# A two-block transformer kernel: the mixer's state space half set among its projections, its retention half behind, and the first attention worked by pairs of heads

## The chip, the cores and the metric

The kernel runs on one core of a Trainium2 chip. The metric is the device time of one execution in microseconds (us); the median of several executions counts. The core's engines each work through a list of instructions in order and wait for one another by semaphores: PE (matrix products; it writes to the accumulation memory PSUM), DVE (vectors), ACT (elementwise functions and copies), POOL (GpSimd, which here adds and multiplies on SBUF alone), and SP (which issues DMA transfers).

## The reference

Two blocks run one after the other on 512 tokens of width 1024, with 256 context tokens beside the second. The first has a causal attention of 8 heads with three dilations (taken here as one mask), a spatial gating unit and a mixture of 32 experts. The second has two layers, each with a mixer and an FFN; the first layer's mixer is the one changed. It joins a retention of 8 heads of 64 with a state space scan (SSD) of 8 heads, both in both directions and in chunks of 128 tokens:

```python
q, k, v, g, z, xbc, dt_raw = jnp.split(h @ w_in, IN0_SPLITS, axis=-1)
...
decay = jnp.exp(jnp.where(lower, cum[..., :, None] - cum[..., None, :], -jnp.inf))
scores = jnp.einsum('bhnid,bhnjd->bhnij', qc, kc) * decay
y_intra = jnp.einsum('bhnij,bhnjv->bhniv', scores, vc)
kv_chunk = jnp.einsum('bhnjd,bhnj,bhnjv->bhndv', kc, to_end, vc)
...
y_inter = jnp.einsum('bhnid,bhni,bhndv->bhniv', qc, jnp.exp(cum), s_before)
...
yr = ((yr - mu) * lax.rsqrt(var + EPS)).reshape(b, l, RET_WIDTH) * gn_w.astype(jnp.float32)
yr = yr.astype(g.dtype) * jax.nn.silu(g)
ys = bhld(y_ssd) + d_skip[:, None] * xs
ys = rms_norm(ys.reshape(b, l, SSD_INNER) * jax.nn.silu(z), ssd_norm_w)
return jnp.concatenate([yr, ys], axis=-1) @ w_out
```

The same scan serves retention (a fixed decay for each head and direction) and SSD (a decay that depends on the token). The context's final states are the latent scan's first ones. The context mixer has two chunks (n = 0, 1), the latent mixer four.

## The kernel before

All is fp32. A large product is made of three passes: an operand is cut into a rounded part `h` (ACT casts, tile `wh`) and a rest `l` (DVE subtracts, tile `wl`, line 240), and `mm3` multiplies h·h, h·l and l·h. `gemm_a` goes through column chunks of 512: for each it cuts four weight tiles, and for each 128 tokens (tt) runs 24 matmuls into one bank `ga`. The ring of cut tiles holds four (`NH`), so that the next chunk's cut waits for the last products of this one. A tile framework's list scheduler turns the program into each engine's order; Python generators that are advanced in turn (`interleave`, `fill`) decide only what it is offered and in which sequence.

*First attention* (`block1`, lines 385 to 425, 86 to 155 us). Head by head, query tile by query tile: the matmul `sc`, DVE's mask and maximum, ACT's exponential with its sum; then one reciprocal per head (L399), four normalising products, ten transposes `tpb`, and after each second head the products `pvb`. `fill(FL[3])` puts three pieces of a conditioning product (`adb`) behind each head. Behind it come the projections of u and v (`ga`).

*Mixer* (class `Mixer`, for the context and for the latent tokens). `proj` makes q, k, v (chunks 0 to 2) and the gates g, z (3 and 4), `rope` turns q and k, `steps` makes the SSD's step sizes and decays. `states` makes every chunk's contribution (`kvr` for retention, `kvsb` for SSD) and `carry` runs them forward and back. `inside(n)` makes both halves' weights and the products with the carried state: `ret_s`, `ssd_x` (the decay's exponent, from masks Rf and Rb), `ssd_s`, `ret_i`, `ssd_i`; `gather(n)` multiplies them with the values (`ret_o`, `ssd_o`) and normalises both halves with one power on POOL (`rs_r`, L290); `turn(n)` transposes the result (`ytb`) and cuts it into `yT`, the out projection's operand. `outputs` runs `inside(n)` ahead of `gather(n-1)`. The weight of an SSD chunk, E, needs four steps: ACT's exponential, DVE's product with `ssd_s`, and on POOL Rb (L1303), Rf (L1304) and E (L1312).

In the latent mixer all projections run first, then `spread`, `states` and `outputs`, then the out projection, whose k runs from 0 to 7 (0 to 3 are retention's columns, 4 to 7 SSD's). The context mixer is filler in the MoE, whose expert weights come in through a ring `mw`: each pair of experts advances it by 2.25 steps.

Of the kernel before, what the change touches and what calls it, by code (L numbers as in the profile page):

```python
# [17 lines left out]
P = 128  # L18
D = 1024
# [132 lines left out]
FL = (0, 1, 1, 3, 1)  # L152
# [6 lines left out]
class K:  # L159
# [91 lines left out]
    def gemm_a(self, xT, tts, kt, wsrc, chunks, ps, tag, bufs, evac, kc=2, nb=512, ahead={}):  # L251

        for n in chunks:
            W = ahead[n]() if n in ahead else [self.wsplit(wsrc(n, c), (kc, nb)) for c in range(kt // kc)]
            for tt in tts:
                bank = ps.tile([P, 512], F32, name="ga", tag=tag, bufs=bufs)
                for kk in range(kt):
                    wh, wl = W[kk // kc]
                    k = kk % kc
                    self.mm3(bank[:, :nb], xT(kk, tt), (wh[:, k, :], wl[:, k, :]), kk == 0, kk == kt - 1)  # L260
                evac(bank[:, :nb], tt, n)
                yield
# [47 lines left out]
    def block1(self, mix):  # L310
# [73 lines left out]
        PTs = {}  # L384
        for h in range(8):
            hp, b0 = h // 2, 64 * (h % 2)
            pr = p1.tile([P, 1280], F32, name="pr", tag="pr", bufs=2)
            mx = p1.tile([P, NT], F32, name="mx", tag="mx", bufs=2)
            ls = p1.tile([P, NT], F32, name="ls", tag="ls", bufs=2)
            for qt in range(NT):  # L390
                n = (qt + 1) * P
                sc = ps.tile([P, 512], F32, name="sc", tag="sc", bufs=2)
                self.mm(sc[:, :n], qT[b0:b0 + 64, hp, qt * P:qt * P + P], kT[b0:b0 + 64, hp, :n], True, True)
                pv = pr[:, OFF[qt]:OFF[qt] + n]
                V.tensor_tensor(pv, sc[:, :n], amask[:, 512 - n:], ALU.add)
                V.tensor_reduce(mx[:, qt:qt + 1], pv, AX, ALU.max, negate=True)
                S.activation(pv, pv, AF.Exp, bias=mx[:, qt:qt + 1], accum_out=ls[:, qt:qt + 1])
            ri = p1.tile([P, NT], F32, name="ri", tag="ri", bufs=2)
            V.reciprocal(ri, ls)  # L399
            for qt in range(NT):  # L400
                pv = pr[:, OFF[qt]:OFF[qt] + (qt + 1) * P]
                V.tensor_scalar(pv, pv, ri[:, qt:qt + 1], None, op0=ALU.mult)
            pt = p1.tile([P, 1280], F32, name="pt", tag="pt", bufs=3)
            PTs[h] = pt
            o = 0
            for jt in range(NT):
# [1746 lines left out]
```

## Time and profile before

| | |
|---|---|
| Median of three runs | 2355.48 us (2351.6 to 2362.92) |
| The profiled execution's own time | 2353.49 us |
| Its span in the trace | 2351.7 us |
| PE busy | 2252.5 us (96%) |
| DVE busy | 1423.6 us (61%) |
| ACT busy | 794.9 us (34%) |
| POOL busy | 442.9 us (19%) |
| Mean DMA rate | 144 GB/s |

Times in the trace count from the span's start. PE's busy time is modelled, since its matmuls overlap: one that stands with 0.39 us may be followed by the next after 0.23. A wait is named by the instruction that ended it.

### The profile page before, as it was taken

To read this page: it belongs to the slowest core of one execution; us is meant where nothing else is said; L and a number is where in the kernel's file an instruction comes from. 1 tells how busy PE (TensorE), PEld (TensorE's weight loads), DVE (VectorE), ACT (ScalarE), POOL (GpSimd) and SP (SyncE) were. 2 spreads that over 40 slices of the span, in tenths; PEclk is the share of its full clock that TensorE was granted. 3 is DMA by queue.
4 is the path that set the end of the run, shared out by engine and by line. 5 is a ranking of instruction groups with operands and counts; after the bars stand their busy time and mean duration, and the time that the engine had idled before them with its cause. 6 is when DMAs were issued, how large, how long until landed. Compare 5 with 4: busy or idle time off the path is not lost.

```text
span 2351.7 us, 30149 instructions
## 1 busy us (share of the span) xinstructions
PE 2252.5 (96%) x11748; PEld 1688.6 (72%) x11748; DVE 1423.6 (61%) x2341; ACT 794.9 (34%) x1382; POOL 442.9 (19%) x331
## 2 busy tenths in 40 slices
PE   9999999999979988899999999989999999999998
PEld 7667755534458756688888888877877668888876
DVE  8766743434475577776677753465568765444446
ACT  4344323222253243342211112134446545222222
POOL 0010310232250256410000000531022123000006
PEclk9999999999989997999999999999999999999999
DMA  8655498998853001344344331221100043332230
GB/s 297 217 183 202 182 373 332 371 389 336 310 197 99 30 28 54 125 152 135 122 139 135 126 108 55 65 97 62 60 1 1 1 147 107 106 99 92 87 106 39
DMA packets 99151, 338.91 MB, mean 144 GB/s; under 512 B 14373, under 2 KB 16293, under 8 KB 99002
## 3 DMA queue, kind: packets, MB, share of 16 engines
q1 hardware_dynamic: 94394, 324.33, 39.1%
q0 software_dynamic: 4608, 12.59, 1.5%
q8 instruction: 94, 1.54, 0.3%
q14 instruction: 55, 0.45, 0.1%
HBM read 323.21 MB, written 17.86 MB: 145 GB/s over the span
## 4 chain that ended last, share of the span: by engine, by line
PE 72%; DVE 8%; issue 3%; POOL 2%; ACT 2%; DMA 0%; POOLq 0%; SPq 0%; DVEq 0%; ACTq 0%
PE gb L243 22%; PE ob L243 14%; PE ga L243 10%; PE cb L243 6%; PE gu L243 5%; PE sc L243 3%; PE yb L243 3%; PE ptb L1808 2%; DVE wl L240 1%; POOL rs_r L290 1%; PE kb L243 1%; PE vb L243 1%; PE ntb L920 1%; PE ssd_x L243 1%; PE tpm L687 1%
## 5 line engine op out<-in xcount | busy, mean ns | idle before, releaser
L239 ACT CAST wh<-wr 128x1024 fp32r<-128x1024 f32 (+1 forms) x239 | 249.1, 1048 | 629.1 <-PE gb L243 274.9
L240 DVE TENSOR_TENSOR wl<-wr,wh 128x1024 fp32r<-128x1024 f32 (+1 forms) x235 | 309.2, 1323 | 216.4 <-ACT wh L239 211.8
L243 PE MATMUL gb<-fh,wh 128*128 128x512 f32 x672 | 264.0, 393 | 0.0
L243 PE MATMUL gb<-fh,wl 128*128 128x512 f32 x672 | 263.9, 393 | 0.0
L243 PE MATMUL gb<-fl,wh 128*128 128x512 f32 x672 | 263.7, 392 | 0.0
L243 PE MATMUL ob<-wh,hidh 128*128 128x512 f32 x440 | 173.9, 395 | 4.4 <-DVE gob L1529 3.0
L243 PE MATMUL ob<-wl,hidh 128*128 128x512 f32 x440 | 172.5, 392 | 0.0
L243 PE MATMUL ob<-wh,hidl 128*128 128x512 f32 x440 | 172.3, 392 | 0.0
L1536 DVE TENSOR_TENSOR acc<-acc,ob 128x512 f32<-128x512 f32 x160 | 108.3, 685 | 84.6 <-PE ob L243 84.6
L860 DVE SCALAR_TENSOR_TENSOR adacc<-wr,cond,adacc 128x512 f32<-128x512 f32 x224 | 152.9, 752 | 1.4 <-DMA wr<-in_w_ada 1.4
L243 PEld LDWEIGHTS gb<-fh,wl 128*128 128x128 f32 x672 | 126.2, 188 | 28.7
L243 PEld LDWEIGHTS gb<-fl,wh 128*128 128x128 f32 x672 | 126.2, 188 | 27.7
L243 PEld LDWEIGHTS gb<-fh,wh 128*128 128x128 f32 x672 | 126.2, 188 | 27.4
L243 PE MATMUL gu<-mw,xgT 128*64 128x512 f32 x512 | 124.3, 600 | 0.7 <-issue 0.7
L243 PE MATMUL cb<-fh,wh 128*128 128x256 f32 x416 | 118.0, 284 | 0.0
L243 PE MATMUL cb<-fl,wh 128*128 128x256 f32 x416 | 117.6, 283 | 0.0
L243 PE MATMUL cb<-fh,wl 128*128 128x256 f32 x416 | 117.0, 281 | 0.0
L1538 POOL TENSOR_TENSOR acc<-acc,gate 128x1024 f32<-128x1024 f32 x10 | 28.1, 2811 | 468.1 <-DVE acc L1536 468.1
L290 POOL TENSOR_TENSOR rs_r<-rs_v,mhalf 128x1 f32<-128x1 f32 (+1 forms) x54 | 46.4, 861 | 336.8 <-DVE rs_v L288 336.5
L243 PEld LDWEIGHTS ob<-wh,hidh 128*128 128x128 f32 x440 | 82.6, 188 | 24.8 <-DVE gob L1529 3.2
L1491 DVE TENSOR_TENSOR sg<-sg,gb 128x512 f32<-128x512 f32 x42 | 28.9, 688 | 112.3 <-PE gb L243 112.2
L243 PEld LDWEIGHTS ob<-wh,hidl 128*128 128x128 f32 x440 | 82.7, 188 | 18.3
(666 smaller groups left out, 4891.3 us busy)
## 6 DMA issues: line engine op xcount, KB each, us to landing
mw<-in_w_gu SPq DMA_DIRECT2D x128, 512.0 KB
wr<-in_w_ada SPq DMA_DIRECT2D x96, 512.0 KB
mw<-in_w_dn SPq DMA_DIRECT2D x64, 512.0 KB
wr<-in_w_fg SPq DMA_DIRECT2D x44, 512.0 KB
wr<-in_w_fu SPq DMA_DIRECT2D x44, 512.0 KB
wr<-in_w_fd SPq DMA_DIRECT2D x44, 512.0 KB
wr<-in_w_ret SPq DMA_DIRECT2D x28, 512.0 KB
wr<-in_w_in SPq DMA_DIRECT2D x19, 512.0 KB
```

The source lines that it names most:

```text
L239: self.nc.scalar.copy(h, src)
L240: (eng or self.nc.vector).tensor_tensor(l, src, h.bitcast(F32), ALU.subtract)
L243: self.nc.tensor.matmul(out, lhsT, rhs, start=start, stop=stop, **kw)
L290: nc.gpsimd.tensor_tensor(r, v, self.mhalf[:, :n], ALU.pow)
L687: nc.tensor.transpose(bank[:, k, :], xg[:, (j * 4 + k) * P:(j * 4 + k + 1) * P], self.ident)
L860: V.scalar_tensor_tensor(acc[:, r], W[:, k], s, acc[:, r], op0=ALU.mult, op1=ALU.add)
L920: nc.tensor.transpose(bank[:, j, i * P:i * P + P], hp[i][:, (2 * kk + j) * P:(2 * kk + j + 1) * P], self.ident)
L1491: nc.vector.tensor_tensor(t, t, out[1], ALU.mult)
L1536: V.tensor_tensor(a[:, sl], a[:, sl], ob, ALU.add)
L1538: G.tensor_tensor(a, a, gate(tt), ALU.mult)
L1808: nc.tensor.transpose(bank[:, qt * P:qt * P + P], prs[h][qt][:, kt * P:kt * P + P], K.ident)
```

## The change

Four things are done. (1) The first attention goes by pairs of heads: both heads' `sc` for one query tile stand next to each other, from the longest tile to the shortest, each tile is normalised at once (32 reciprocals), and the transposes (`spread`) and products (`values`) of the pair before stand among the scores of this one. (2) The mixer is split into `ssd()` and `ret()`. (3) In `ret()` both directions lie on the partitions, 64 and 64: k and q are doubled with their decays (`kd` on DVE, `qd` on POOL), the state takes 8 products of 64 columns per chunk, its carry runs forward on POOL and back on DVE, and the product with the carried state is added in PSUM to that with the values, 16 matmuls `ret_o` for a chunk. (4) In the latent mixer `ssd()` is offered among the projections, 2.25 steps to each 128 tokens; the SSD columns are turned, then retention runs; the out projection's k begins with the SSD columns. The masks and E go to a ring of their own of four tiles (`sw`), and the ring `b9` shrinks from 7 tiles to 5.

```diff
-FL = (0, 1, 1, 3, 1)
+FL = (0, 1, 1, (2, 2, 1, 1), 1)
...
+        def scores(p, qt):
+            n = (qt + 1) * P
+            sc = [ps.tile([P, 512], F32, name="sc", tag=tag, bufs=2) for tag in ("sc", "mm")]
+            for c in range(2):
+                r = slice(64 * c, 64 * c + 64)
+                self.mm(sc[c][:, :n], qT[r, p, qt * P:qt * P + P], kT[r, p, :n], True, True)
+            for c in range(2):
...
+                V.tensor_tensor(pv, sc[c][:, :n], amask[:, 512 - n:], ALU.add)
+                V.tensor_reduce(mx, pv, AX, ALU.max, negate=True)
+                S.activation(pv, pv, AF.Exp, bias=mx, accum_out=ls)
+                V.reciprocal(ls, ls)
+                V.tensor_scalar(pv, pv, ls, None, op0=ALU.mult)
...
+        for p in range(5):
+            for i in range(NT):
+                if p < 4:
+                    scores(p, NT - 1 - i)
+                    fill(FL[3][i])
+                if p and i:
+                    spread(p - 1, i - 1)
+                    if i > 1:
+                        values(p - 1, i - 2)
+            if p:
+                spread(p - 1, 3)
+                for jt in (2, 3):
+                    values(p - 1, jt)
...
+        kd = self.doubled(V, "kd", self.k, n, K.kdec)
+        b = self.pst("kvr", "sc")
+        for h in range(8):
+            K.mm(b[:, h * 64:h * 64 + 64], kd[:, h * P:h * P + P], self.v[:, n * 512 + h * 64:n * 512 + h * 64 + 64], True, True)
...
+    def carry_r(self, n, d):
...
+        r = slice(64 * d, 64 * d + 64)
+        E = self.nc.vector if d else self.nc.gpsimd
...
+    def ssd(self):
...
+        for n in range(nt):
...
+            for h in range(8):
+                S.mul(Rf[:, h, :], K.m_le, self.dt[:, n, 0, h:h + 1])
+            G.tensor_tensor(Rb, K.m_gt[:, None, :].to_broadcast([P, 8, P]), self.dt[:, n, 1, :, None].to_broadcast([P, 8, P]), ALU.mult)
+            G.tensor_tensor(Rf, Rf, Rb, ALU.add)
...
+            G.tensor_tensor(E, E, Rf, ALU.mult)
...
+    def ret(self):
...
+            qd = self.doubled(G, "qd", self.q, n, K.qdec)
+            qdT = work("qdT")
+            for hb in range(2):
+                bank = pst("qtb", "tp")
+                for h in range(4):
+                    self.nc.tensor.transpose(bank[:, h * P:h * P + P], qd[:, (4 * hb + h) * P:(4 * hb + h) * P + P], K.ident)
+                S.copy(qdT[:, hb * 512:hb * 512 + 512], bank)
+            yield
+            ob = pst("ret_o", "sc")
+            for h in range(8):
+                o = ob[:, h * 64:h * 64 + 64]
+                K.mm(o, PT[:, h, :], self.v[:, n * 512 + h * 64:n * 512 + h * 64 + 64], True, False)
+                K.mm(o, qdT[:, h * P:h * P + P], self.SBr[:, n, h * 64:h * 64 + 64], False, True)
...
+            V.tensor_reduce(st, ob3, AX, ALU.add)
+            V.tensor_scalar(st, st, 1.0 / 64, None, op0=ALU.mult)
+            V.tensor_tensor(yr3, ob3, st[:, :, None].to_broadcast([P, 8, 64]), ALU.subtract)
+            S.activation(sq, yr, AF.Square)
+            V.tensor_reduce(rr, sq3, AX, ALU.add)
+            rs = K.rstd(rr, self.pool, 8, 1.0 / 64, 1e-6)
+            V.tensor_tensor(yr3, yr3, rs[:, :, None].to_broadcast([P, 8, 64]), ALU.mult)
+            V.tensor_tensor(gn, yr, gn, ALU.mult)
+            if self.lat:
+                self.turn(n, 0)
+            yield
...
+LF = 2.25
...
-        for n in ("smx", "ropew", "q", "k", "v", "xst", "qT", "kT", "wro", "SBs0", "SBs1"):
-            where[n] = (plb, "b9", 7)
...
+        for n in ("q", "k", "xst", "qT", "kT", "SBs0", "SBs1"):
+            where[n] = (plb, "b9", 5)
...
+        def half():
+            yield from lm.steps()
+            yield from lm.ssd()
+        fill = half()
+        interleave(lm.proj(range(3)), fill, LF)
+        run_gen(fill)
...
+        for n in range(NT):
+            lm.turn(n, 1)
...
+        run_gen(lm.ret())
...
-        run_gen(lm.out(res, gt, normed, {0: lambda: wo}))
+        run_gen(lm.out(res, gt, normed, {0: lambda: wo}, ks=[4, 5, 6, 7, 0, 1, 2, 3]))
```

How the engines' orders move is seen at four places; a row is one instruction or a run of like ones (their count behind x), with its line, output, operands and size.

PE in the first attention, before: the second head's scores, one tile after the other from short to long, and then the transposes `tpb` of the head ahead of it.

```order
L243 MATMUL sc<-kT,qT 128x128
L243 MATMUL adb<-wr,cond 32x128 x5
L243 MATMUL sc<-kT,qT 128x256
L243 MATMUL sc<-kT,qT 128x384
L243 MATMUL adb<-wr,cond 32x128 x7
L243 MATMUL sc<-kT,qT 128x512
L243 MATMUL adb<-wr,cond 32x128 x3
L409 MATMUL tpb<-c_ident,pr 128x128
```

At that place in the change, from the second pair's first tile on (`res` is the room of a pair's second head).

```order
L243 MATMUL sc<-kT,qT 128x512
L243 MATMUL adb<-wr,cond 32x128 x9
L243 MATMUL sc<-kT,qT 128x384 x2
L243 MATMUL sc<-kT,qT 128x256
L416 MATMUL tpb<-c_ident,pr 128x128 x4
L416 MATMUL tpb<-c_ident,res 128x128 x4
L243 MATMUL sc<-kT,qT 128x256
L416 MATMUL tpb<-c_ident,pr 128x128 x3
```

Scores of a pair stand beside each other, and the transposes of the pair ahead stand among them. In the latent mixer PE's order before has, for the third chunk, both halves' products together, with the transposes `ytb` of the first chunk between:

```order
L243 MATMUL ssd_s<-bcT 128x128 x2
L243 MATMUL ret_i<-SBr,qT 128x128 x8
L243 MATMUL ssd_i<-SBs_7021,bcT 128x512
L1404 MATMUL ytb<-c_ident,res 128x128 x8
L243 MATMUL ssd_i<-SBs_7021,bcT 128x512
L243 MATMUL ret_o<-v,PT 128x64 x8
L243 MATMUL ssd_o<-xst,E 128x64 x8
```

In the change, PE's rows for the SSD chunk n=1, from its second half of `ssd_x` on, which stand between the second weight chunk's last projection matmul and the third's first:

```order
L243 MATMUL ssd_x<-Rf,c_m_gt 128x512
L243 MATMUL ssd_x<-Rb,c_ustrict_2688 128x512
L243 MATMUL ssd_s<-bcT 128x128 x2
L243 MATMUL ssd_i<-SBs_6730,bcT 128x512 x2
L1438 MATMUL ytb<-c_ident,res 128x128 x4
L243 MATMUL ssd_o<-xst,E 128x64 x8
L243 MATMUL ga<-wh,ah_5646 128x512
```

The products of retention are gone from between `ssd_x` and `ssd_o`; projection matmuls stand on both sides. DVE at the third weight chunk's cuts (`wl`), in the change:

```order
L1359 TENSOR_TENSOR ys<-ssd_o,sint 128x512
L1360 TENSOR_TENSOR ys<-ys,sint 128x512
L1361 TENSOR_TENSOR ys<-ys,res 128x512
L240 TENSOR_TENSOR wl<-wr,wh 128x1024
L289 TENSOR_SCALAR rs_v<-frs 128x1
L1365 SCALAR_TENSOR_TENSOR res<-ys,rs_r,ynw 128x512
L240 TENSOR_TENSOR wl<-wr,wh 128x1024
L1278 TENSOR_TENSOR Rf<-c_utri_2682,latla 128x1024
L240 TENSOR_TENSOR wl<-wr,wh 128x1024 x2
```

Before, no SSD chunk's work stood among these cuts. Last, PE in the second part of the latent mixer in the change, from the end of one chunk's `ret_o` to the start of the next (`qtb` are the transposes of `qd`):

```order
L243 MATMUL ret_o<-v,PT 128x64
L243 MATMUL ret_s<-qT,kT 128x128 x8
L1438 MATMUL ytb<-c_ident,res 128x128 x4
L1402 MATMUL qtb<-c_ident,qd 128x128 x8
L243 MATMUL ret_o<-SBr,qdT 128x64
```

The chunk's `ytb` has moved ahead of the next chunk's `ret_o`; before, `ret_o` and `ssd_o` of the next chunk or two stood ahead of it.

## Rows read from the trace of the kernel before

**Rows 1.** The page's part 4: chain of waits, share of the span by engine.
```profile
PE 72%; DVE 8%; issue 3%; POOL 2%; ACT 2%; DMA 0%; POOLq 0%; SPq 0%; DVEq 0%; ACTq 0%
```

**Rows 2.** Windows by stage: us, busy time (x instructions) by engine, PE clock, DMA.
```profile
86.00:155.00 69.00, 69.00 (x596) 38.03 (x595) 49.13 (x125) 37.30 (x98) 0.00 (x0) 1.00 0.59 200
...
762.00:836.00 74.00, 73.27 (x352) 58.16 (x351) 40.19 (x79) 17.55 (x24) 15.13 (x18) 1.00 0.08 24
...
836.00:959.00 123.00, 100.23 (x507) 72.59 (x506) 99.51 (x152) 47.65 (x128) 78.26 (x48) 0.83 0.17 60
...
959.00:1005.00 46.00, 39.27 (x174) 30.55 (x173) 34.32 (x48) 22.60 (x39) 21.61 (x15) 0.91 0.29 103
```

**Rows 3.** DVE groups, 80 to 160: xcount, busy us, mean ns, idle before.
```profile
L399 DVE RECIPROCAL ri<-ls 128x4 f32<-128x4 f32 x8 | 1.4, 171 | 1.0 <-ACT pr L397 1.0
...
L240 DVE TENSOR_TENSOR wl<-wr,wh 128x1024 fp32r<-128x1024 f32 x4 | 4.8, 1221 | 0.0
```

**Rows 4.** Timeline of PE, end of the first attention: start, length, instruction.
```profile
146.56 0.73 PE L243 MATMUL ga<-wh,xTh 128*128 128x512 f32 x2
...
154.44 0.50 PE L243 MATMUL ga<-wl,xTh 128*128 128x512 f32 x1
```

**Rows 5.** Timeline of PE, latent projections: first matmul, first of the last 24.
```profile
762.54 0.39 PE L243 MATMUL ga<-wh,ah 128*128 128x512 f32 x1
...
829.77 0.39 PE L243 MATMUL ga<-wh,ah 128*128 128x512 f32 x1
```

**Rows 6.** Timeline of the latent mixer: transposes, `kvsb`, one chunk's work.
```profile
835.22 1.03 PE L1156 MATMUL mtb<-c_ident,xsT 128*128 128x128 f32 x8
...
848.83 3.70 PE L243 MATMUL kvsb<-xsd,bt 128*128 128x512 f32 x8 [0.24 <-DVE SBr L1209]
...
875.92 1.12 PE L243 MATMUL ssd_x<-Rf,c_m_gt 128*128 128x512 f32 x2
...
879.70 1.90 POOL L1303 TENSOR_TENSOR Rb<-c_m_gt,latdt 128x1024 f32<-128x1024 f32 x1 [2.21 <-PE ssd_x L243]
...
880.00 1.16 PE L243 MATMUL ret_i<-SBr,qT 64*128 64x128 f32 x16
...
881.09 1.98 PE L243 MATMUL ssd_i<-SBs,bcT 128*128 128x512 f32 x4
...
882.91 1.89 PE L243 MATMUL ret_o<-v,PT 128*128 128x64 f32 x16
...
884.64 1.95 PE L243 MATMUL ssd_o<-xst,E 128*128 128x64 f32 x16
...
884.99 2.35 POOL L1312 TENSOR_TENSOR E<-E,Rf 128x1024 f32<-128x1024 f32 x1
```

**Rows 7.** Timeline of the normalisation: square, waiting transposes, power.
```profile
890.90 0.63 ACT L1366 ACTIVATE sq<-ycat 128x512 f32<-128x512 f32 x1 [8.90 <-DVE ycat L1365]
...
900.36 1.97 PE L1404 MATMUL ytb<-c_ident,res 128*128 128x128 f32 x8 [6.10 <-DVE res L1373]
...
942.02 1.80 POOL L290 TENSOR_TENSOR rs_r<-rs_v,mhalf 128x9 f32<-128x9 f32 x1
```

**Rows 8.** Windows in the latent mixer, columns as in rows 2.
```profile
865.00:876.00 11.00, 5.96 (x29) 3.13 (x25) 10.15 (x13) 0.84 (x3) 8.48 (x6) 0.53 0.00 0
...
896.00:916.00 20.00, 15.64 (x62) 12.47 (x63) 13.90 (x22) 3.91 (x12) 10.69 (x7) 0.50 0.08 27
```

**Rows 9.** Timeline of PE: first out-projection matmul, last transposes of the mixer.
```profile
937.69 0.77 PE L243 MATMUL ga<-wh,yT 128*128 128x512 f32 x1
...
958.55 0.66 PE L1404 MATMUL ytb<-c_ident,res 128*128 128x128 f32 x2 [3.52 <-DVE res L1373]
```

**Rows 10.** Groups of instructions on DVE, 835 to 960.
```profile
L1244 DVE TENSOR_TENSOR SBs<-SBs,stt 128x512 f32<-128x512 f32 x6 | 9.6, 1611 | 0.1
...
L1311 DVE TENSOR_TENSOR E<-E,ssd_s 128x512 f32<-128x512 f32 x8 | 5.2, 679 | 6.2 <-PE ssd_s L243 6.2
```

**Rows 11.** Window in the MoE, columns as in rows 2.
```profile
560.00:570.00 10.00, 10.00 (x69) 6.38 (x69) 7.67 (x17) 2.42 (x5) 1.14 (x1) 1.00 0.44 158
```

More of the change, by code (lines that the diff above doesn't have):

```diff
@@ L249, in mm3, with gemm_a @@
         self.mm(out, A[1], Bm[0], False, stop, **kw)
-    def gemm_a(self, xT, tts, kt, wsrc, chunks, ps, tag, bufs, evac, kc=2, nb=512, ahead={}):
+    def gemm_a(self, xT, tts, kt, wsrc, chunks, ps, tag, bufs, evac, kc=2, nb=512, ahead={}, ks=None):
+        ks = ks or list(range(kt))
         for n in chunks:
@@ L383, in block1 @@
         amask = self.load_const("amask", p1)
[L384 to L406, printed above, removed]
@@ L407, in block1, with spread @@
+        def spread(p, jt):
+            o, w = sum((NT - j) * P for j in range(jt)), (NT - jt) * P
+            for c in range(2):
+                if jt == 0:
+                    PTs[p, c] = p1.tile([P, 1280], F32, name="pt", tag="pt", bufs=3)
                 bank = ps.tile([P, 512], F32, name="tpb", tag="tp", bufs=2)
@@ new lines, in ends, with doubled @@
+    def ends(self, pairs):
+        for t, f in pairs:
+            if self.lat:
+                self.nc.vector.tensor_copy(t, f)
+            else:
+                self.nc.vector.memset(t, 0.0)
+    def doubled(self, eng, name, t, n, dec):
+        o = self.work(name)
+        eng.tensor_tensor(o.rearrange("p (h d e) -> p h d e", d=2, e=64),
+                          t[:, n * 512:n * 512 + 512].rearrange("p (h o e) -> p h o e", o=1, e=64).to_broadcast([P, 8, 2, 64]),
+                          dec[:, :, :, None].to_broadcast([P, 8, 2, 64]), ALU.mult)
+        return o
@@ L1376, in outputs @@
-    def outputs(self, ahead=None):
-        K = self.K
-        if self.lat:
-            ynw = K.bcast(self.I["ynw"], D, K.wp, "ynw", "wr", K.NR)
-        else:
-            ynw = K.spread_row(K.w4("ynw"), self.I["ynw"], lambda: self.pst("ynb", "sc"))
-        o = {}
-        self.masks = {0: self.mask(0)}
-        for n in range(self.nt + 1):
-            if n < self.nt:
-                o[n] = yield from self.inside(n)
-                if n == self.nt - 1 and ahead:
-                    ahead()
-                yield
-            if n >= 1:
-                self.gather(n - 1, o.pop(n - 1), ynw)
-                if self.lat:
-                    self.turn(n - 1)
-                yield
@@ L1408, in out @@
-    def out(self, hs, gt, done=None, ahead={}, plain=(0,), join=True):
+        self.spread_x()
+        yield
+        st = [self.big(f"SBs{j}") for j in range(2)]
+        hn = nt // 2
+        self.SBs = lambda n: st[n // hn].rearrange("p (t g d c) -> p t g d c", t=hn, g=2, d=2)[:, n % hn]
+        self.ends(((self.SBs(0)[:, :, 0], K.fin_s[:, :, 0]), (self.SBs(nt - 1)[:, :, 1], K.fin_s[:, :, 1])))
+        for n in range(nt):
+            self.kv_ssd(n)
+            yield
+        self.weights_row()
@@ L1945, in scan @@
                 yield
-            yield from cm.spread()
-            yield from cm.states()
-            yield from cm.outputs()
+            yield from cm.ssd()
+            yield from cm.ret()
             for n in range(NC_):
-                cm.turn(n)
+                for hb in range(2):
+                    cm.turn(n, hb)
             yield
```

420 lines of the change are left out of this document (193 added, 227 removed).

## The prediction

> **What bounds the kernel now.** I read the page's chain of waits first: the matrix engine (PE) holds 72% of it [rows 1], so only a stage where PE waits, or does work it could leave out, can give time back. The table by stage [rows 2] then shows three such stretches among those the change touches. In the first attention (86 to 155 us) PE is never idle, yet its work there is small operands and filler, and the vector engine (DVE) is busy 49 of 69 us. In 762 to 836 PE runs the latent q, k, v projections without a gap (73.3 of 74). In 836 to 959, the latent mixer proper, PE is busy 100 of 123 at a granted clock of 0.83 and DVE 99.5; its 23 us of idle PE are the slack there is.
>
> The timelines give the marks. The projections start at 762.54, and the last 24 of their 288 matmuls `ga` stand from 829.77 to the first transposes at 835.22 [rows 5, 6], 0.227 us each. In the tail, PE waits 6.10 us for the eight transposes `ytb` of n=0 (from 894.3 to 900.4) [rows 7], and the clock is 0.50 from 896 to 916 and 0.53 from 865 to 876 [rows 8], that is, at the lower of its two levels. The out projection begins at 937.69, and the last `ytb` comes at 958.55, when 62 of the 192 out-projection matmuls are done [rows 9].
>
> **The change part by part.** *First attention.* The same masks, maxima, exponentials and products, but the 8 reciprocals of 128x4 become 32 of 128x1: 24 x 0.17 = 4.1 us more DVE work, against 49.1 [rows 2, 3]. The gain is order. The two heads of a pair stand on different row halves, so their score matmuls can run together, as `ret_i` shows: 16 instructions on alternating halves in 1.16 us [rows 6]. And DVE always finds another head's row to work on. Were DVE fed without a gap from 87 us, its 53.2 us, four weight cuts `wl` of 1.22 among them [rows 3], would end at 140; I take 141.5 for the scores and cuts, and the first 24 `ga` of the next projection are then done by about 150. Now the first stands at 146.56 and 26 are done at 154.44 [rows 4], where 44 would be: 18 x 0.227 = **-4 us**. Bounds: 0 (DVE still idles as long as now) and -8.
>
> *Context mixer, filler in the MoE.* There the weight DMA is the limit as long as PE takes the experts' weights; from 560 to 570 PE does mixer work in their place and the DMA share is 0.44 at 158 GB/s [rows 11]. Those 5.6 us are the most to win there. The new order has more PE work (16 `ret_o` matmuls per n instead of 8 and 8 `ret_i`, 1.73 x 2 against 1.73 + 1.09 [rows 6]), ends one pair of experts earlier, and waits in other places. **-1**, bounds -6 and +5.
>
> *Latent, first part: the whole SSD half among the projections.* To the 72.7 us of projection (762.5 to 835.2) come, per n, `ssd_x` with `ssd_s` 4.08 (875.92 to 880.00), `ssd_i` 1.82 and `ssd_o` 1.9 [rows 6], 4 x 7.8 = 31.1; eight `kvsb` 2 x 3.70; 24 transposes at 1.03 for eight, 3.1 [rows 6]. Sum 114.3: with no wait the last `ga` would end at 876.9. But PE works in order, and `ssd_o` needs E, which GpSimd (POOL) makes through Rb, Rf and E: from Rb's start at 879.70, just behind `ssd_x`, to E's end at 887.34 is 7.6 us [rows 6]. What stands between on PE covers it for n=0 (24 `ga` 5.4, `ssd_s` some 0.5, `ssd_i` 1.8), n=2 and n=3. For n=1 nothing but `ssd_s`, `ssd_i` and four `ytb` stands there (the order ahead of this), 2.8 us: a wait of 5. Before the second and third weight chunks DVE reaches the cuts only behind SSD work (behind the states' carries; behind the three adds and products of n=1, which themselves wait for that `ssd_o`): 0 to 6 us each, I take 3 each, which is two cuts and a product of 0.68 [rows 3, 10]. So 11 us of waits and the last `ga` at **888**.
>
> *Latent, second part: retention.* The `rint` scalings and adds are gone. In front stand 32 `kvr` at 0.22 (`ret_o`'s rate), 32 transposes and 12 `ytb`, about 13 us, with four kd, each as wide as a cut (1.22), copies and the backward carry on DVE beside it, about 18 with them; then the first 16 `ret_o` (3.5): 23 us. After that each n runs a chain that nothing covers. PE's order has `ytb` of n ahead of the transposes `qtb` and `ret_o` of n+1. So between them lie DVE's reduce, scale, subtract, ACT's square (0.63), reduce, rs_v, POOL's rs_r (1.80), two products: 5 x 0.68 [rows 10], two small ones of 0.17 like the reciprocal [rows 3], 0.63, 1.80 [rows 7] and 0.9 for eight hand-overs make 7.1 us, then `ytb` 0.5, `qtb` 1.0, the copy 0.6, `ret_o` 3.5: 12.7 us each for three n, and 7.6 for the last. Sum 23 + 38 + 7.6 = **68**, ending at 956. Behind n=2 and n=3 out-projection matmuls fill the wait, as the first halves of their sums need only the SSD result; in PE's order 47 stand ahead of the last `ytb`, against 62 now, a debt of 15 x 0.227 = 3.4. So 956 + 3.4 against 958.6: **+1**.
>
> So of the 23 idle us of PE little is won: 11 us of waits stand in the first part, and in the second a serial chain of 7 us per n, where before the chunks of both halves overlapped.
>
> *What speaks against it in the skill.* Row: DVE's adds of two SBUF operands beside POOL take 1.61 us, where the products with one PSUM operand of the same shape take 0.68 [rows 10]. The Trainium skill, GPSIMD Engine Reference, section Specifications, says that GpSimd shares its SBUF interfaces with VectorE and contends with VectorE instructions of two SBUF inputs; the trace agrees. The cuts that PE waits for in the first part are of that kind. [...]
>
> **The sum.** -4 - 1 + 1 = -4. From the profiled 2353.5 that is 2349.5; the profiled execution lies 2.0 under the median of the three runs, so a median by the same steps is 2351. A difference under 0.5% (11.8 us) can hardly be told from none in this kernel.
>
> **The rivals.** *The waits aren't there (faster).* E may come early where POOL is free, and the cuts may find DVE free: then the last `ga` ends at 877 (-11); kd and the carries of the first chunks may be done before, and the head of the second part falls by 6; attention gives its -8. -4 - 11 - 6 - 4 = -25, from either 2353.5 or 2355.5: **2328 to 2331**. For it: from 762 to 1005 PE's modelled work is 213 of 243 us [rows 2], so about 26 are there to win and no more. Against it: in an engine that works in order the wait of n=1 can't be passed by the matmuls behind it.
>
> *PE falls to its lower clock (slower).* Every wait of 5 to 6 us in the tail now is followed by a stretch at 0.50 to 0.53 [rows 7, 8]; in 896 to 916 PE gets its 15.6 us of work through at half speed, so some 7 us are lost behind one wait. The Trainium skill, TensorE: Matmul & The Clock Gate, section HAM oscillation, describes the same pattern of short work between waits that never regains the clock; the trace agrees. If the three waits of the first part cost 4 each so (+12), and in the second part n=1 and n=2 run `ytb`, `qtb` and `ret_o` at half rate (2 x 5) with the head slower by 3 (+13): -4 + 25 = +21, **2374 to 2376**. It slows the kernel past the 0.5% where the last `ytb` comes after some 972 (958.6 + 11.8 + 5 of attention and context, less the 3.4).
>
> *It moves work and nothing else (same).* Attention gives 0, since the exponentials and transposes set its pace; the context mixer's new waits cost the DMA 5: **2358 to 2360**.
>
> **How the numbers follow.** The forecast (2340 to 2358, latent mixer even, attention a few us) 0.35; the last rival 0.07; the waits that aren't there 0.36; the clock 0.22. The forecast's lower end passes the 0.5% bound (2343.7) with some 0.04 of its chance. So faster 0.40, same 0.38, slower 0.22. The range runs from 2328 to 2376, the two rivals' prices; the forecast's own is 2340 to 2358. Between the two sums I give **2350**.
>
> **What would show it.** In the changed kernel: the first `ga` after the attention by 145 us, with 44 done at 154.4. The last projection `ga` near 888 (877: the first rival; 898: the clock), and a PE wait of some 5 us at the second chunk's `ssd_o` released by POOL's E. Four `ytb` in the second part, each released by DVE's product with `gn` some 7 us after `ret_o`, and spaced by 12 to 13 us; the last at 956. A granted clock under 0.6 in these stretches speaks for the slower rival. The prediction is wrong if projections and SSD work run without PE idle, or if the retention's chunks turn out to overlap, or if the FFN's first matmul `cb` moves by other than the last `ytb` does.

## The result, and the profile after

The changed kernel takes 2425.23 us (median of 4 runs, 2422.58 to 2429.83) where the kernel before takes 2356.28 (4 runs, 2351.6 to 2362.92): a ratio of 1.0293, 95% interval 1.0263 to 1.0322. It is slower by 69 us, outside the range of 2328 to 2376. The profiled execution took 2425.33 us, with a span of 2423.6 (before: 2351.7).

The chain of waits of the changed kernel barely moves against [rows 1]:

```profile
PE 71%; DVE 7%; issue 4%; POOL 2%; ACT 2%; DMA 1%; POOLq 0%; SPq 0%; DVEq 0%; ACTq 0%
```

The place shows in the windows by stage, columns as in [rows 2]. The first four are the windows of [rows 2], the last three this kernel's own stages: the first part from the first projection `ga` to the last, the second to the last `ytb`, and the tail to the FFN's first `cb`:

```profile
86.00:155.00 69.00, 68.21 (x627) 35.50 (x626) 51.65 (x153) 39.07 (x100) 0.00 (x0) 1.00 0.64 214
762.00:836.00 74.00, 58.72 (x246) 40.12 (x245) 45.21 (x79) 22.09 (x42) 12.77 (x12) 0.86 0.11 36
836.00:959.00 123.00, 104.91 (x471) 80.68 (x469) 85.71 (x102) 42.50 (x99) 65.54 (x42) 0.85 0.11 35
959.00:1005.00 46.00, 32.91 (x158) 30.73 (x158) 17.07 (x25) 5.65 (x10) 7.03 (x4) 0.50 0.07 24
...
773.00:928.00 155.00, 128.28 (x514) 89.28 (x513) 95.97 (x145) 51.98 (x120) 63.23 (x45) 0.88 0.14 45
928.00:1021.00 93.00, 71.86 (x397) 65.33 (x395) 49.62 (x62) 17.18 (x29) 25.65 (x17) 0.65 0.11 40
1021.00:1074.00 53.00, 41.23 (x182) 31.73 (x180) 36.92 (x47) 22.16 (x39) 24.32 (x18) 0.90 0.31 109
```

From 762 to 836 PE was busy throughout before and is now idle for 15 us; from 959 to 1005 it runs at the lower clock. The marks of one profiled run of each kernel, read as first and last starts of the matmuls of a tile, give the lengths of the stages (all in us; "first `gu`" is where the experts begin, "experts" reaches to the last `gu`, "part 1" from the first latent `ga` to the last, "part 2" to the last `ytb`, "tail" to the first `cb`). In the kernels with the old latent mixer part 1 is the projections and part 2 the whole mixer. Single marks scatter: PE's order up to the first `gu` is the same in all kernels with the new attention, and yet that mark stands anywhere from 299.5 to 307.8:

```
kernel       median   first gu  experts  part 1  part 2  tail   sum of the three
before       2356.28    304.5    308.1    72.5   125.1   44.2   241.8
after        2425.23    303.6    319.4   154.7    93.3   52.8   300.8
e1_att       2345.23    299.5    308.4    72.4   124.7   44.3   241.4
e2_ctx       2362.70    307.9    320.4    72.3   130.7   40.0   243.0
e3_lat       2407.49    304.9    308.5   157.5    91.7   52.4   301.6
e5_attctx    2358.83    300.7    323.4    72.3   130.9   40.0   243.2
e6_ring      2408.39    300.8    324.9   132.7    95.0   53.1   280.8
e7_rope      2406.89    302.2    321.6   134.8    97.4   53.5   285.7
e8_seq       2425.42    300.4    323.4    83.0   164.7   52.7   300.4
e9_sw        2399.35    300.7    321.6   134.6    88.7   53.0   276.3
e4_late      2402.60    300.2    324.1   153.1    67.3   52.1   272.5
e13_two      2382.76    299.8    321.7   134.2    69.9   52.3   256.4
e10_three    2387.28    306.5    324.3   132.2    77.0   54.6   263.8
e12_attlat   2365.56    301.8    311.0   130.6    70.7   54.5   255.8
e14_pad      2419.39    307.8    322.9   152.5    89.7   51.8   294.0
e15_cheap    2353.91    300.0    316.4    72.4   130.8   40.0   243.2
```

Of the 71.9 us between the two spans the latent stage holds 59.0 and the experts' stage 11.3; the rest nearly cancels. What PE waits for in part 1 (engine, tile, line, releaser: us, times, longest):

```profile
PE kvsb L243 <- DVE xsd L1241: 12.1, 2, 8.9
PE ssd_o L243 <- POOL E L1334: 11.3, 3, 6.1
PE ga L243 <- ACT wh L239: 1.4, 1, 1.4
```

And from SP's list from 740 on the loads of raw weights and of the row of norm weights, first in the kernel before, then in the changed one (start, time from the first issue to the last, load, count):

```profile
743.10 46.11 SPq L223 DMA_DIRECT2D wr<-in_w_ret  x7
...
849.07 0.38 SPq L192 DMA_DIRECT2D ynw<-in_ynw  x1
```

```profile
742.68 0.33 SPq L223 DMA_DIRECT2D wr<-in_w_ret  x1
804.03 0.33 SPq L192 DMA_DIRECT2D ynw<-in_ynw  x1
822.45 66.92 SPq L223 DMA_DIRECT2D wr<-in_w_ret  x8
```

Where seven loads of raw weights were issued between 743 and 789, one is now, and the next begins at 822. SP's own waits in the changed kernel, from 740 to 1060, say why:

```profile
...
SPq L223 <- DVE ys L1360: 70.0, 4, 35.3
SPq L192 <- DVE q L1165: 60.9, 1, 60.9
SPq L223 <- DVE wl L240: 28.3, 4, 15.1
SPq L223 <- DVE q L1165: 18.0, 1, 18.0
```

The ring of six tiles for raw weights, which held the row of norm weights before too, now also holds the mixer's work tiles but Rf, Rb and E: the rope's `ropew`, and of the SSD half `xsd`, `sts`, `sint` and `ys` (the account of the change names only the ring of the masks and E). SP issues in order: it stood 60.9 us until a rope tile was free (its last reader is the add into `q`, L1165) to load `ynw`, and the weights stood behind that load, another 18.0 us for the next rope tile.

How the ring reaches PE shows in the timeline of the changed kernel ahead of its longest wait:

```profile
803.47 0.42 DVE L1165 TENSOR_TENSOR q<-ropew 128x256 f32<-128x256 f32 x1
803.80 2.49 DVE L1241 TENSOR_TENSOR xsd<-xst,latex 128x512 f32<-128x512 f32 x4
...
816.92 0.58 ACT L1141 COPY q<-ga 128x512 f32<-128x512 f32 x1 [4.63 <-PE ga L243]
...
819.36 5.73 POOL L1414 TENSOR_TENSOR res<-res,ynw 128x512 f32<-128x512 f32 x4
819.43 1.47 DVE L1164 TENSOR_TENSOR q<-ropew 128x256 f32<-128x256 f32 x1 [0.61 <-POOL ropew L1163]
820.83 1.48 DVE L1165 TENSOR_TENSOR q<-ropew 128x256 f32<-128x256 f32 x1
822.23 4.62 DVE L1241 TENSOR_TENSOR xsd<-xst,latex 128x512 f32<-128x512 f32 x4
...
825.79 6.17 PE L243 MATMUL kvsb<-xsd,bt 128*128 128x512 f32 x8 [8.91 <-DVE xsd L1241]
```

The rope of the last `q` tile stands ahead of the second half of `xsd` in DVE's list and waits for that tile's projection; next in PE's list is `kvsb`, which waits for `xsd`. The late row's four products on POOL fall there too: beside them the add into `q` takes 1.48 us where it took 0.42 and four `xsd` 4.62 where they took 2.49. The second weight chunk's first `ga` follows at 833.37, behind `kvsb` and a wait of 1.4 us for its cut. So it is by `xsd` that the ring costs PE most; for the weights themselves PE waits 1.9 us in this part.

### The profile page after: what moved, and what is told of

Same layout as the page of the kernel before. It is cut to its first block, busy times and chain, and to the rows that moved or that the text cites. A ratio compares the mean times of both kernels' runs of the same rounds, so it can differ in the third digit from the quotient of the medians.

```text
span 2423.6 us, 30296 instructions
## 1 busy us (share of the span) xinstructions
PE 2290.7 (95%) x11844; PEld 1715.9 (71%) x11844; DVE 1438.4 (59%) x2330; ACT 800.5 (33%) x1379; POOL 440.0 (18%) x327
## 4 chain that ended last, share of the span: by engine, by line
PE 71%; DVE 7%; issue 4%; POOL 2%; ACT 2%; DMA 1%; POOLq 0%; SPq 0%; DVEq 0%; ACTq 0%
PE gb L243 21%; PE ob L243 14%; PE ga L243 10%; PE cb L243 6%; PE gu L243 5%; PE sc L243 3%; PE yb L243 2%; PE ptb L1842 2%; DVE wl L240 1%; PE ret_o L243 1%; POOL rs_r L291 1%; PE kb L243 1%; PE vb L243 1%; PE ssd_x L243 1%; PE ssd_o L243 1%
## 5 line engine op out<-in xcount | busy, mean ns | idle before, releaser
L243 PE MATMUL gu<-mw,xgT 128*64 128x512 f32 x512 | 132.0, 599 | 2.5 <-DMA mw<-in_w_gu 1.0
L1525 DVE TENSOR_TENSOR sg<-sg,gb 128x512 f32<-128x512 f32 x42 | 28.9, 688 | 114.3 <-PE gb L243 114.2
```

Of the source, the lines that this page charges most:

```text
L243: self.nc.tensor.matmul(out, lhsT, rhs, start=start, stop=stop, **kw)
L1525: nc.vector.tensor_tensor(t, t, out[1], ALU.mult)
```

## The experiments

**The parts alone.** e1_att keeps the new `block1`, e2_ctx the new context mixer, e3_lat the new latent mixer, each beside the old rest; e5_attctx the first two. Where old and new mixer meet, the context's final states are copied into the other's layout. The edit of e1_att (`MixerOld` is the class of the kernel before, with its old calls):

```diff
-        cm = Mixer(k, "ctx", psm, pcx, c4, k.work, dict(tp=CX, mm=CX, dt=CX, sc=[CX]))
+        cm = MixerOld(k, "ctx", psm, pcx, c4, k.work, dict(tp=CX, mm=CX, dt=CX, sc=[CX]))
...
-        lm = Mixer(k, "lat", psl, plx, big, k.work, dict(tp=TP, mm=B6, dt=B6, sc=[B6]))
+        lm = MixerOld(k, "lat", psl, plx, big, k.work, dict(tp=TP, mm=B6, dt=B6, sc=[B6]))
```

> The first attention by pairs alone, both mixers as before. In the changed kernel's trace the work behind the attention stands 1.5 us earlier than before, so if the parts add up this one gives -1 to -2 us (2354 to 2355). The rival, that the pairs' order costs time that shows later (their filler, or the room in the residual's tile), would give +5 or more.

> The context mixer alone in the new order, first attention and latent mixer as before (a copy of 4 small pieces puts the final retention state into the old layout, and its room is a tile of the raw-weight ring). If the 10 us by which the last expert product is later in the changed kernel come from the mixer's new order among the experts, +10 to +12 (2367). If they come from the attention's changed filler or from the weight transfers' state at the stage's start, 0 to +3.

> The latent mixer alone in the new order (SSD among the projections, retention behind), the rest as before, with four small copies for the state. If the parts add up: from the start of the latent projections to the FFN's first product the changed kernel takes 301 us where before it took 242, so +59 to +62 (2415 to 2418). If the latent mixer suffers from what the context mixer left behind, less than +50.

> The new first attention and the new context mixer together, the latent mixer as before. Alone they gave -12 us and +6 us, so if the parts simply add, 2351 us (2347 to 2356). The three parts alone sum to +44 us where the whole change costs +69; if these two disturb each other (the attention's gain lost in the expert stage, whose weight transfers are the limit), the missing 25 us stand here and the time is 2365 to 2375. If it is 2351, they stand between these two and the latent mixer.

Measured against before: e1_att 0.9951 (0.9932 to 0.997), e2_ctx 1.0025 (1.0007 to 1.0043), e3_lat 1.0206 (1.018 to 1.0232), e5_attctx 1.0009 (0.9991 to 1.0027). The attention is a gain of 12 us (7 to 16 by the interval), more than either reading of the expectation, and the kernel with it alone beats both kernels. The latent stage is as long in e3_lat (301.6) as in the whole change (300.8), so no interaction with the others shows there. By medians the attention gives 12 us alone and 4 beside the new context mixer (e2_ctx to e5_attctx); whether the two interact is not shown, since the marks scatter by more: the experts' stage ends at 607.9 in e1_att and at 612.8 in e12_attlat, which have the same attention and context mixer. By medians the latent mixer costs 50 alone and 66 on top of e5_attctx, by the marks 58 to 60 in both. e3_lat's profiled run is its slowest (2413.63), 6 us over its median; the rest of the difference is left open.

**The first latent part.** e9_sw moves the rope's tile to the ring of Rf, Rb and E:

```diff
-        lm.work = lambda name: plb.tile([P, 1024], F32, name=name, tag="sw", bufs=4) if name in ("Rf", "Rb", "E") else k.w4(name)
+        lm.work = lambda name: plb.tile([P, 1024], F32, name=name, tag="sw", bufs=4) if name in ("Rf", "Rb", "E", "ropew") else k.w4(name)
```

e6_ring has this too, and loads the row of norm weights in two halves; e7_rope has both and puts the rope off; e8_seq has none of them, but the SSD behind the projections:

```diff
-            self.ynw = K.bcast(self.I["ynw"], D, K.wp, "ynw", "wr", K.NR)
+            self.yns = K.bcast(self.I["ynw"], 512, K.wp, "ynw", "wr", K.NR, 512)
...
+            self.ynr = K.bcast(self.I["ynw"], 512, K.wp, "ynr", "wr", K.NR)
```

```diff
-                if self.lat:
-                    self.rope(dst[n], tt)
...
-                if n == 0 and self.lat:
-                    self.rope(dst[n], tt)
+                if n == 2 and self.lat:
+                    for t in (dst[0], dst[1]):
+                        self.rope(t, tt)
```

```diff
-        fill = half()
-        interleave(lm.proj(range(3)), fill, LF)
+        fill = lm.steps()
+        interleave(lm.proj(range(3)), fill, 0.5)
         run_gen(fill)
+        run_gen(lm.ssd())
```

> The whole change, with the rope's work tiles in the ring of Rf, Rb and E in place of the raw weights' ring, and the row of norm weights loaded in two halves, the retention's half only when retention begins. Theory (late weights and GpSimd's early products res x ynw in the first latent part are what holds its vector engine): the gap in the weight transfers from 772 to 800 us goes, the four 5.7 us products leave that part, and it takes 135 to 145 us in place of 155; time 2405 to 2415. Rival (the vector engine's order alone, with rope ahead of xsd, makes the wait of 8.9 us, and the weights come in time anyway): the part stays at 150 to 155 and the time at 2420 to 2428.

> As the run with the rings, and the rope of the q and k tiles put off until v's tiles are projected, so that on the vector engine no rope stands ahead of xsd and of the first states. Theory of the vector engine's order: the two waits of kvsb on xsd (12.1 us) go, and some us at the lower clock with them; against the run with the rings alone another 12 to 20 us less, the first latent part 125 to 135 us. Rival: the waits only move to the last chunk of weights, where rope now stands beside the SSD work: no gain, or up to 5 us more.

> The whole change, but the SSD half behind the projections instead of among them. If work between the projections in in-order engines is what costs, the projections run in some 75 us as before and the SSD half alone takes 55 to 65 (four chunks of 10 to 12, states 12, transposes 4): the first part 130 to 140 in place of 155, time 2402 to 2412. If the interleaving does gain something (projections cover the waits for E and the adds), the SSD half alone takes over 80, at the lower clock, and the time is 2425 or more.

> The whole change with only the rope's work tiles moved out of the raw weights' ring; the row of norm weights stays whole, so GpSimd's four early products res x ynw stay in the first latent part. It splits the 17 us that the two edits together gave. If late weights are the cause (ring), most of it is here: 2408 to 2414, first part 133 to 140 us. If GpSimd's products beside the vector engine are, 2418 to 2425, first part 148 to 155 us.

e9_sw alone gives 1.0188 (1.0163 to 1.0213), 26 us less than the change; part 1 falls from 154.7 to 134.6. In its trace SP's load of the row and the weights come earlier, all eight `xsd` stand ahead of the third rope on DVE, and of PE's waits on `xsd` none is left:

```profile
769.11 0.33 SPq L192 DMA_DIRECT2D ynw<-in_ynw  x1
806.62 62.16 SPq L223 DMA_DIRECT2D wr<-in_w_ret  x8
```

```profile
792.76 4.91 DVE L1241 TENSOR_TENSOR xsd<-xst,latex 128x512 f32<-128x512 f32 x8
...
800.25 1.48 DVE L1164 TENSOR_TENSOR q<-ropew 128x256 f32<-128x256 f32 x1 [0.61 <-POOL ropew L1163]
```

```profile
PE ssd_o L243 <- POOL E L1334: 10.8, 2, 9.7
PE kvsb L243 <- ACT bt L1238: 4.4, 2, 4.1
```

So the rope's place in the ring is the cause of most of it. Whether by the order of `xsd` or by the weights' lateness the run doesn't separate, as both moved: the next weights still start 34 us after the part does (49 in the change), and hold PE up through ACT, whose cast waits 2.9 us for them with the copy of `bt` behind it: PE waits 4.1 for that copy. POOL's four products, 5.83 us together, still stand in this part of e9_sw, now behind `xsd`; taking them out (e6_ring) shortens the part by only 1.9 us more, to 132.7. e6_ring (1.0214, 1.0178 to 1.025) gains no more in time: moved to the second part, the products stand there, and `kvr` waits 9.4 us for kd where it waited 2.8. e7_rope (1.0212, 1.018 to 1.0245) gained nothing, as its rival said; but it had little to win, since with the ring freed no `xsd` stands behind the third and fourth rope any more. e8_seq (1.03, 1.0267 to 1.0334) is as slow as the change: parts 1 and 2 together are 247.7 against 248.0, so with the ring as it was, setting the SSD half among the projections neither gained nor lost. The SSD half behind the projections with the ring freed was not run.

**The second part.** e4_late turns a chunk only behind the next chunk's `ret_o`; e14_pad leaves the program's order and adds six matmuls that nobody reads per chunk:

```diff
-            if self.lat:
-                self.turn(n, 0)
+            if self.lat and n:
+                self.turn(n - 1, 0)
             yield
+        if self.lat:
+            self.turn(nt - 1, 0)
```

```diff
             if self.lat:
+                for i in range(6):
+                    K.mm(pst("pad", "sc"), K.ident, self.v[:, 0:512], True, True)
                 self.turn(n, 0)
```

> The whole change, but a chunk's retention result is turned after the next chunk's ret_o, so that the normalisation chain (8 us from the end of ret_o to ytb in the changed kernel) no longer stands between two chunks' products. If that chain sets the pace of the second part, it shrinks from 93 us by 3 x 6 to 8 and by what the clock gives back: -20 to -30 (2395 to 2405). If the second part is bound by ret_o and DVE's and POOL's own work, -5 at most.

> The whole change, and behind each chunk's ret_o six extra 128x512 matmuls whose result nobody reads, so that the matrix engine has work while it waits for the chain. If the lower clock is what stretches the second part from the forecast 68 to 93 us, the granted clock there rises from 0.5 towards 1.0, ytb, qtb and ret_o run at full rate, and the part takes 75 to 82 us although it holds more work: time 2408 to 2416. If the steps of the chain themselves are longer, the part stays at 93 or grows by the added work (6 x 1.0 us per chunk at the lower clock, some of it in the wait): 2425 to 2435.

e4_late: 1.0196 (1.0176 to 1.0216), 23 us less, with part 2 at 67.3 in place of 93.3. The chain is there, as forecast, but a step of it is longer. One chunk in the changed kernel:

```profile
958.50 0.69 PE L243 MATMUL ret_o<-SBr,qdT 128*128 128x64 f32 x2
...
965.20 0.69 DVE L1417 TENSOR_REDUCE fst<-ret_o 128x8 f32<-128x512 f32 x1 [7.02 <-PE ret_o L243]
...
968.55 1.65 POOL L291 TENSOR_TENSOR rs_r<-rs_v,mhalf 128x8 f32<-128x8 f32 x1 [16.63 <-DVE rs_v L289]
970.18 1.89 POOL L1216 TENSOR_TENSOR qd<-q,qdec 128x1024 f32<-128x1024 f32 x1
970.23 2.39 DVE L1423 TENSOR_TENSOR yr<-yr,rs_r 128x512 f32<-128x512 f32 x1 [1.76 <-POOL rs_r L291]
...
973.49 1.09 PE L1438 MATMUL ytb<-c_ident,res 128*128 128x128 f32 x4 [5.90 <-DVE res L1424]
...
977.07 0.53 PE L243 MATMUL ret_o<-SBr,qdT 128*128 128x64 f32 x2
...
983.61 0.69 DVE L1417 TENSOR_REDUCE fst<-ret_o 128x8 f32<-128x512 f32 x1 [7.09 <-PE ret_o L243]
```

From `fst` to `ytb` 8.3 us, on to the first `ret_o` 3.6, `ret_o` itself 6.5: 18.4. The clock in this stretch is 0.50 ([rows 8] had the same in the shorter tail). In e14_pad windows of the second part are partly back at the higher level:

```profile
965.00:975.00 10.00, 6.91 (x52) 5.08 (x50) 3.29 (x6) 1.25 (x3) 2.56 (x2) 0.97 0.01 2
975.00:985.00 10.00, 7.84 (x41) 6.00 (x41) 4.00 (x5) 1.76 (x3) 0.96 (x1) 0.69 0.16 52
985.00:995.00 10.00, 6.19 (x36) 3.64 (x36) 5.49 (x7) 0.74 (x2) 3.51 (x2) 0.99 0.00 0
```

There 16 `ret_o` take 3.5 us (965.59 to 969.09) against 6.7, but PE's order has moved too: the next chunk's first `ret_o`, which waits 5.2 us for DVE's `PT`, and two of the padding matmuls stand ahead of `ytb`, so that `fst` to `ytb` takes 10.4 us there against 8.3. `fst` to `fst` is 17.0, 16.3 and 13.8 us against 18.4, 18.3 and 12.3. The time, 1.0271 (1.0239 to 1.0302), is not clear of the change's interval, and part 2, 89.7, lies between the two expectations. The lower clock explains about 3 us per chunk in `ret_o`; that the wait in the chain is the order's is shown by e4_late.

**Together.** e13_two has the edits of e9_sw and e4_late. e10_three has those of e6_ring and e4_late, and loads the out projection's second weights earlier; e12_attlat has the same latent mixer with the old context mixer:

```diff
         close("plb")
+        raw1 = [k.wraw(I["w_ro"][1, c], (2, 512)) for c in range(4)]
```

> The whole change with two mends only: rope's work tiles out of the raw weights' ring (-26 alone) and the turn of a chunk behind the next chunk's ret_o (-23 alone). If they add: 2425 - 49 = 2376, with the stage from the projections' start to cb at 250 us (before 242). If they lean on the same slack: 2388 or more.

> The whole change with three mends: both edits of the rings (-17), the turn of a chunk put behind the next chunk's ret_o (-23), and the out projection's second weights loaded before the residual is reloaded (the tail from the last ytb to cb took 53 us against 44, so -8). If they add: 2425 - 48 = 2377, still slower than before. If the second and the third lean on the same slack (the tail only starts earlier, and waits the longer for its weights), 2385 to 2390.

> The new attention, the old context mixer, and the new latent mixer with the three mends. Latent stage by the measured parts: 301 - 22 - 26 - 8 = 245 us from the projections' start to cb, against 242 before; with the attention's -12, 2345 + 3 = 2348 (2343 to 2356). If the latent mixer with its mends is as good as the old one, this tells that the new order was not bad in itself but in what it queued behind; if it is over 2360, the order itself costs.

e13_two: 1.0123 (1.009 to 1.0156), 42 us under the change, where the two alone give 26 and 23: they nearly add. What remains against before is 14.6 us in the latent stage and 13.6 in the experts'. e10_three is no better (1.0127, 1.0094 to 1.016): the early loads only turn the tail's wait into one on ACT's `wh` (12.4 us), and it carries e6_ring's wait on kd (9.0). e12_attlat is 1.0057 (1.0036 to 1.0077), 20 us above e1_att, the old latent mixer with the same attention; it has the wait on kd too (9.5). No mend tried makes the new latent order as good as the old one.

**The context mixer.** e11_rate takes 1.7 steps of mixer work for each step of the experts in place of 2.25; e15_cheap leaves out the `ret_o` on the carried state and its transposes. Both have the old latent mixer:

```diff
-        interleave(k.moe(p4, psm, ahead, got), fill, 2.25)
+        interleave(k.moe(p4, psm, ahead, got), fill, 1.7)
```

```diff
-            for hb in range(2):
+            for hb in range(2 if self.lat else 0):
...
-                K.mm(o, PT[:, h, :], self.v[:, n * 512 + h * 64:n * 512 + h * 64 + 64], True, False)
-                K.mm(o, qdT[:, h * P:h * P + P], self.SBr[:, n, h * 64:h * 64 + 64], False, True)
+                K.mm(o, PT[:, h, :], self.v[:, n * 512 + h * 64:n * 512 + h * 64 + 64], True, self.lat == 0)
+                if self.lat:
+                    K.mm(o, qdT[:, h * P:h * P + P], self.SBr[:, n, h * 64:h * 64 + 64], False, True)
```

> The new attention and the new context mixer with the old latent mixer, but 1.7 in place of 2.25 steps of mixer work to each step of the experts. Theory: with 2.25 the new order puts more matrix work per expert than the weight transfers cover (from 520 to 560 us PE is busy to 97 to 100% and the DMA share falls to 0.77), so spread thinner the expert stage falls from 323 us to some 310 and the time from 2359 to 2346 to 2350. Rival: the new mixer's own work is longer and no spreading helps; the stage stays at 319 to 324 us.

> New attention and new context mixer, latent mixer as before; in the context mixer the product with the carried state (32 ret_o) and its 16 transposes qtb are left out, so the retention's carried part is missing from the context's result. Before, ret_o and ret_i took 7.0 us of the matrix engine in the expert stage, with the change ret_o takes 12.4 and qtb 2.8. If this extra work is the price, the stage falls by 8 to 10 us, from 323 to 313 to 315, and the time from 2359 to 2349 to 2351. If the price is in the order (what waits for what, and when the transfers get their room), the stage falls by 4 us at most: 2354 or more.

e11_rate went against its theory: 1.008 (1.0056 to 1.0103), the stage 336.7 us. e15_cheap: 0.9997 (0.9983 to 1.0012), the stage 316.4 in place of 323.4 in e5_attctx. So 7 of the 15 us by which the stage of e5_attctx is longer than that of e1_att (308.4) follow the additional matrix work, its waits included; by the medians it is 5. The windows from 520 to 560 before, in the changed kernel, and in e15_cheap (its second half):

```profile
520.00:540.00 20.00, 20.00 (x89) 7.30 (x89) 5.18 (x10) 5.76 (x12) 7.27 (x7) 1.00 1.01 374
540.00:560.00 20.00, 19.92 (x110) 9.75 (x106) 6.82 (x12) 3.55 (x7) 10.44 (x7) 1.00 1.00 385
```

```profile
520.00:540.00 20.00, 19.43 (x109) 10.10 (x107) 9.50 (x13) 3.88 (x7) 10.07 (x8) 1.00 0.78 277
540.00:560.00 20.00, 20.00 (x109) 10.72 (x109) 6.61 (x12) 2.60 (x5) 2.44 (x2) 1.00 0.78 279
```

```profile
540.00:560.00 20.00, 17.60 (x73) 7.24 (x70) 9.18 (x18) 2.67 (x5) 3.33 (x2) 0.91 0.66 234
```

Before, PE was as full as the DMA queues; with the new order it is still full, and the DMA share has fallen. In e15_cheap neither is full there, which speaks against PE's work for the other 8 us; what they are was not found.

## Why the prediction was wrong

**First attention: the 4 us held by the marks.** The first `ga` starts at 144.15 (forecast by 145, [rows 4]). From the first `sc` (86.53, now 87.99) to the first `ga` it is 56.2 us where it was 60.0, to the 48th 72.3 where it was 75.5, and in every kernel with the new attention the same: 3.2 us against 4. The other sign, 44 `ga` done at 154.4, failed: there are 22, and before there were 15, where the prediction read 26 in the rows. What the rest of the 12 us in the median of e1_att is, no run shows.

**Context mixer: the sign was wrong.** I gave -1 because the dip at 560 us [rows 11] seemed to be won back. The step that failed is taking the weight DMA for the only limit of that stage. PE was as full (19.92 and 20.00 of 20 us above), so additional PE work there counted. I had put that work at 0.64 us per n (1.73 x 2 against 1.73 + 1.09) and left out the transposes; it was 8.2 us for both n (`ret_o` 12.4 against 7.0 for `ret_o` and `ret_i`, and 2.8 for `qtb`). The stage lost 11.3 us, beyond the +5 that I took for the bound.

**First part: 888 was forecast for the last `ga`, which is 125.5 us after the start; it took 154.7.** Of these PE was busy for 128.0, against 114.3 in the sum, and idle for 26.7, against 11. The wait for E at n=1 held (5 forecast, 6.1 measured); the sum took n=0 as covered, and there PE waited 4.1. The 6 us for the cuts were 1.9. The step that failed is a wait that the sum put at nothing: its `kvsb` stand at 2 x 3.70, and none of its 11 us of waits is theirs. They waited 12.1 us for `xsd`, whose tiles shared a ring with the rope's. I had costed each step on PE, DVE, ACT and POOL, but not a ring whose members had changed, neither what it does to DVE's order nor to SP's list, which I took as having the weights present. The second term that failed is PE's work, taken at the full clock: the granted clock is 0.88 over the part and 0.73 from 800 to 830. The slower rival had 4 us for each of three waits. e9_sw gives 20.1 of the 29.2 us back, 11.0 in idle time and 9.0 in PE's work, at a clock of 0.92:

```profile
772.20:906.90 134.70, 118.98 (x513) 84.39 (x512) 94.83 (x143) 51.01 (x120) 63.02 (x44) 0.92 0.14 47
```

The last 9 lie in the waits for E (10.8 us there, 9.7 of them in one piece) and for `bt` (4.4), and in the stretches at the lower clock that are left.

**Second part: 68 forecast, 93.3 measured.** The shape was right: `ytb` of the first two chunks waits 11.6 us in all for DVE's product with `gn`, and behind the other two out-projection matmuls fill most of the wait. Two terms were mis-sized. The head took 37.5 us (from 927.7 to the first `fst`) and not 23: DVE had the SSD tail of the last chunk, two weight cuts and the copies of the final states ahead of and among the kd products, the first 16 `ret_o` took 6.7 for 3.5 at the lower clock, and these copies, which I had not listed, took 1.99 and 4.13 us beside POOL. The chain took 18.4, 18.3 and 12.3 us and not 12.7 each: `ret_o` 6.5 for 3.5 at the lower clock, the product with `rs_r` 2.39 for 0.68 in the first two, `ytb` to `ret_o` 3.6 for 2.1. The rival "PE falls to its lower clock" had this mechanism, but at 13 us for the part it priced half of what came. It took its price from a tail whose clock came back behind each wait (1.00 from 876 to 896 in the kernel before); here it stayed at 0.50 from 954 to 1004, through three chunks.

**The product of 2.39 us.** In two chunks it starts with POOL's qd and takes 2.39 and 2.38; in the two where POOL is idle the same instruction takes 0.69:

```profile
988.58 2.38 DVE L1423 TENSOR_TENSOR yr<-yr,rs_r 128x512 f32<-128x512 f32 x1 [1.76 <-POOL rs_r L291]
...
1019.11 0.69 DVE L1423 TENSOR_TENSOR yr<-yr,rs_r 128x512 f32<-128x512 f32 x1 [1.75 <-POOL rs_r L291]
```

The Trainium skill, GPSIMD Engine Reference, section Specifications, names contention of GpSimd with VectorE instructions that have two SBUF inputs, as this product has; the trace agrees, with a loss of 1.7 us beside POOL's 1.89. The prediction looked for it at the weight cuts of the first part only.

**Tail: 52.8 us against 44.2.** SP's reload of the residual waits for the last chunk's product, and the out projection's second weights, issued at 949.69 before, are issued at 1021.68 behind it. Loading them first did not help (e10_three), so what else holds the tail is open. That `cb` moved by 69.5 us where the last `ytb` moved by 62 is one of the prediction's own signs of being wrong.

## What to carry to other kernels

When work moves past a DMA queue, list who shares the queue's ring of tiles before and after: a small tile that lives long in that ring holds up the loads behind it and the other engines' work tiles, and no table of engine times shows this. A serial chain on the matrix engine costs more than its steps at full rate: take the steps from rows at the lower clock, and put the next chunk's independent work ahead of the wait in program order. Try a change's parts alone, since here one part is worth 12 us and stood inside a loss of 69. And read a stage from a mark of its own start: from the first `sc` the attention's gain is the same 3.2 us in every trace, while the first `gu` scatters by 8.

## What the runs showed of the hardware that was not expected

A copy on DVE with a single SBUF source also stretches beside POOL, and not for one of its instructions but for its whole run of them. In the changed kernel two copies of 128x512 take 0.75 us while POOL is idle; the final states' copies of 64x512 take 1.99 and 4.13, and the longer one ends 0.3 us after POOL's run of three instructions (at 931.77) does:

```profile
782.85 0.75 DVE L1209 COPY SBs<-fin_s 128x512 f32<-128x512 f32 x2
...
925.84 1.99 DVE L1209 COPY SBr<-fin_r 64x512 f32<-64x512 f32 x1
927.92 4.13 DVE L1209 COPY SBr<-fin_r 64x512 f32<-64x512 f32 x1
```

```profile
927.91 1.03 POOL L1260 TENSOR_TENSOR str<-SBr,rtot 64x512 f32<-64x512 f32 x1 [0.36 <-DVE rs_v L289]
928.91 0.54 POOL L291 TENSOR_TENSOR rs_r<-rs_v,mhalf 128x1 f32<-128x1 f32 x1
929.43 2.34 POOL L240 TENSOR_TENSOR wl<-wr,wh 128x1024 fp32r<-128x1024 f32 x1
```

In e6_ring, where POOL's run goes on through the row's four products, the same copy takes 9.01 us. The copies of 64x512 out of PSUM that follow take 0.67 to 0.68.

Extra matmuls in the gaps bring the granted clock from 0.50 to 0.69 to 0.99 and halve `ret_o` (e14_pad), yet the time falls by 6 us at most, which the noise could also give, while the order of e4_late gives 23 with stretches still at 0.50.
